# Post-norm multiplication of the last MLP quarter on GpSimd, and the last product's weight forms emitted earlier, in a two-layer decoder trunk

## The chip, the cores and the metric

One core of a Trainium2 chip. The metric is the time of one execution on the device, in microseconds (us), as the median of several executions; the profile is of one execution more.

## What is computed

Two layers of a decoder trunk on 512 tokens of width 1024, all in f32. Each layer is a token mixer (two attention groups on one input projection), a cross-attention into 256 memory tokens and an MLP, and each of the three has a norm in front and a norm behind, the latter added to the residual. The change lies in the last of the three and in what follows it:

```python
def rms_norm(x, g):
    y = xf * lax.rsqrt(jnp.mean(xf * xf, axis=-1, keepdims=True) + EPS)
    return (y * g.astype(jnp.float32)).astype(x.dtype)
...
for l in range(DEPTH):
    ...
    hdn = jnp.square(jax.nn.relu(rms_norm(x, pre_mlp_g[l]) @ w_up[l]))
    x = x + rms_norm(hdn @ w_down[l], post_mlp_g[l])
```

`w_up` is 1024 x 4096 and `w_down` 4096 x 1024.

## The kernel before

Every f32 matmul is made of three matmuls of a shorter type: each operand is split into a high part and a low rest (`whi` and `wlo` for weights, `fh` and `fl` for hidden values, `xth` and `xtl` for normalised tokens). ScalarE writes the high part, VectorE subtracts it from the source to get the rest. A raw weight tile `raw` holds two row blocks of 512 columns, so its split takes one ScalarE and one VectorE instruction of 1024 columns (L164, L165); weights of an input projection are also scaled by a norm's vector (L192, L197). There are 8 buffers for `raw` and 5 each for `whi` and `wlo`.

The tokens are 4 tiles of 128 rows (`t` from 0 to 3), the width is 2 halves of 512 columns (`n` 0 and 1). The MLP runs over 4 quarters of the hidden width (`qd_`). A quarter first computes its hidden values, then multiplies them with `w_down` by a scheme of seven products in place of eight. Product `p` needs a left form (sums of hidden blocks, `left_forms`) and two right forms, one for each `g` (differences of weight tiles, `right_form`: for product 4 one VectorE subtraction of 1024 columns at L1039, and then the split). A product is 24 matmuls into two PSUM tiles (`wa`, `wc` or `we`, one for each `j`), and `finish` adds these on VectorE into the accumulators `acc[t][n]` (L1107). In the last quarter the products run in the order 1, 2, 5, 6, 3, 7, 4:

```python
plan = ((1, A, True, False, ((0, 0),)), (2, E, True, True, ((0, 0),)),
        (5, C, True, False, ((2, 1),)), (6, A, False, False, ((0, 1),)),
        (3, C, False, True, ((0, 1),)), (7, A, False, True, ((2, 1), (2, 0))),
        (4, E, True, True, ((2, 0),)))
```

There a half of a row tile is complete after product 2 (tiles 0 and 1, left half), 3 (tiles 0 and 1, right), 7 (tiles 2 and 3, right) and 4 (tiles 2 and 3, left). `done(t, n)` then takes the sum of squares of the half on ScalarE (L372, tile `junk`) and multiplies the half by the post-norm's vector `gb[n]`, a 128x512 tile (L1045). When both halves of a tile are there, `add_post_norm` forms `pnm` from the two sums (L420, VectorE), raises it to the power -0.5 on GpSimd (`pnr`, L139; called the root below) and adds the scaled halves to the residual `xs` (L423, VectorE). In the last layer these go to the output; in the first they are stored in DRAM and normalised for the next layer (`norm_x`: squares, a root `n1r`, and `xn` on GpSimd and ScalarE), transposed on TensorE (`tp`) and used by the next input projection (`ptm`).

The right forms of the last product are made in a list of their own, `last_w`, after the matmuls of product 7 in the program's text.

The order in which each engine runs its instructions is set by the scheduler of the language from the program's text: an earlier place in the text gives priority, and an instruction that can't run yet lets others pass. Each engine then runs its own list strictly in order.

Of the kernel before, what the change touches and what calls it, by code (L numbers as in the profile page):

```python
# [16 lines left out]
OP = mybir.AluOpType  # L17
# [6 lines left out]
NT = S // 128  # L24
# [21 lines left out]
def block_kernel(ctx: ExitStack, tc, x, mem, positions, rel_bias, w_in, q_norm_g, w_uq, kv_norm_g,  # L46
# [3 lines left out]
    nc = tc.nc  # L50
# [38 lines left out]
    def store_x(t, dst):  # L89
        for n in range(2):  # L90
            nc.sync.dma_start(dst[t * 128:(t + 1) * 128, n * 512:(n + 1) * 512], xs[t][n])
# [274 lines left out]
    def feat_major(*a, **k):  # L366
        run(feat_major_steps(*a, **k))

    def sumsq(src, ss, scale=1.0):
        w = src.shape[-1]  # L370
        junk = unit("junk", (128, w))
        nc.scalar.activation(junk, src, AF.Square, scale=scale, accum_out=ss)  # L372
# [20 lines left out]
    def norm_x(h, lo, t, tag, help=None):  # L393

        hv = (h[:, 0:4, :], h[:, 4:8, :])
        lv = (lo[:, 0:4, :], lo[:, 4:8, :]) if SPLIT else (None, None)
        ms = small(tag + "ms", 2)
        for n in range(2):
            sumsq(xs[t][n], ms[:, n:n + 1], scale=1.0 / 32.0)
        r = row_rstd((ms[:, 0:1], ms[:, 1:2]), tag)  # L400
        xns = []
        for n in range(2):
            xn = unit("xn")
            if n == 1 and help is nc.scalar:
                nc.scalar.activation(xn, xs[t][n], AF.Copy, scale=r[:, 0:1])
            else:
                eng = nc.gpsimd if n == 0 or help is None else help
                eng.tensor_scalar(xn, xs[t][n], r[:, 0:1], 1.0, op0=OP.mult, op1=OP.mult)
            xns.append(xn)
        put_off(("xt", t), DELAY, lambda: [transposed(xns[n], n, list(zip(hv, lv)), t) for n in range(2)])  # L410

    def new_xt():
        h = xtp.tile([128, NK, S], WD, tag="xt", name="xth")
        l = xtp.tile([128, NK, S], WD, tag="xt", name="xtl") if SPLIT else None
        return h, l

    def add_post_norm(ys, ms, t, dst=None):

        m = small("pnm", 1)
        nc.vector.scalar_tensor_tensor(m, ms[:, 0:1], EPS, ms[:, 1:2], op0=OP.add, op1=OP.add)  # L420
        r = rpow(m, "pn")
        for n in range(2):
            nc.vector.scalar_tensor_tensor(xs[t][n], ys[n], r[:, 0:1], xs[t][n], op0=OP.mult, op1=OP.add)  # L423
            if dst is not None:
                (nc.sync, nc.scalar)[n].dma_start(dst[t * 128:(t + 1) * 128, n * 512:(n + 1) * 512], xs[t][n])
# [136 lines left out]
    for l in range(DEPTH):  # L562
# [437 lines left out]
        acc = [[None, None] for _ in range(NT)]  # L1000
        ss = [small("mss", 2) for _ in range(NT)]
        nxh = nxl = None
        gb = None

        def left_forms(F, ra, rb):

            a11, a21 = ra[:, :, 0:256], ra[:, :, 256:512]
            a12, a22 = rb[:, :, 0:256], rb[:, :, 256:512]

            def part(p, src):  # L1010
                h, lo = unit("fh", (128, 2, 256), WD), unit("fl", (128, 2, 256), WD)
                split_from(h, lo, src)
                F[p].append((h, lo))

            s1, s2 = unit("s1", (128, 2, 256)), unit("s2", (128, 2, 256))
            part(1, a11)
            nc.vector.tensor_add(s1, a21, a22)
            part(5, s1)
            nc.vector.tensor_sub(s2, s1, a11)
            part(6, s2)  # L1020
            part(2, a12)
            nc.vector.tensor_sub(a21, a11, a21)
            part(7, a21)
            nc.vector.tensor_sub(a12, a12, s2)
            part(3, a12)
            part(4, a22)
# [15 lines left out]
        def done(t, n):  # L1042

            sumsq(acc[t][n], ss[t][:, n:n + 1], scale=1.0 / 32.0)
            nc.vector.tensor_mul(acc[t][n], acc[t][n], gb[n])  # L1045
            ready_halves[t] += 1
            if ready_halves[t] < 2:
                return
            add_post_norm(acc[t], ss[t], t, out[0] if l == DEPTH - 1 else None)
            if l < DEPTH - 1:  # L1050
                store_x(t, xsave)
                norm_x(nxh, nxl, t, "n1", help=nc.scalar)
# [3 lines left out]
        for qd_ in range(4):  # L1056
            if qd_ == 3 and l < DEPTH - 1:
                nxh, nxl = new_xt()
            F = {p: [] for p in range(1, 8)}
            for g in range(2):  # L1060
                ra = pp.tile([128, 1280], F32, tag="P", name="ra", bufs=2)[:, 0:1024]
                rb = pp.tile([128, 1280], F32, tag="PT", name="rb", bufs=2)[:, 0:1024]
                ra, rb = [r.rearrange("p (k c) -> p k c", k=2) for r in (ra, rb)]

                def ev_up(m, ps, ra=ra, rb=rb):
                    r = (ra, rb)[m // 2][:, m % 2, :]
                    nc.scalar.activation(r, ps, AF.Relu)
                    nc.scalar.activation(r, r, AF.Square)

                feat_major(w_up[l], (qd_ * 2 + g) * 512, 4, NK, G_MLP + 8 * l, xh_f, xl_f, S, ev_up,  # L1070
                           whole=2 if qd_ == 0 and g == 0 else 0)
                left_forms(F, ra, rb)
            B = [[raw_w(w_down[l], qd_ * 1024 + g * 512 + r * 256, 2, n * 512, 512)
                  for r in range(2) for n in range(2)] for g in range(2)]
            A = [pss.tile([128, 512], F32, tag="s", name="wa") for _ in range(2)]
            C = [pst.tile([128, 512], F32, tag="t", name="wc") for _ in range(2)]
            E = [None] * 2
            end = qd_ == 3


            plan = ((1, A, True, False, ((0, 0),)), (5, C, True, False, ((2, 1),)),
                    (6, A, False, False, ((0, 1),)), (2, E, True, True, ((0, 0),)),
                    (7, A, False, False, ((2, 1),)), (3, C, False, True, ((0, 1),)),
                    (4, A, False, True, ((2, 0),)))
            if end:
# [4 lines that stand above are left out]
            for p, ps, first, last, dsts in plan:  # L1090
                if ps is E:
                    E[:] = [mm_ps("we") for _ in range(2)]

                def product(g, i, j, w):
                    c = slice(j * 128, (j + 1) * 128)
                    fh, fl = F[p][g]
                    mm(ps[j], fh[:, i, c], fl[:, i, c], w[0][:, i, :], w[1][:, i, :],
                       first and g + i == 0, g + i == 2, not first)

                def finish(j):  # L1100
                    for d, n in dsts:
                        t = d + j
                        if acc[t][n] is None:
                            acc[t][n] = unit("acc")
                            nc.vector.tensor_copy(acc[t][n], ps[j])  # L1105
                        else:
                            nc.vector.tensor_add(acc[t][n], ps[j], acc[t][n])  # L1107
                        if end and p in (2, 3, 4) or end and p == 7 and n == 1:
                            done(t, n)

                if end and p == 4:
                    for j in range(2):
                        for g in range(2):
                            for i in range(2):
                                product(g, i, j, last_w[g])
                        finish(j)
                        flush()
                    continue
                for g in range(2):
                    w = right_form(p, B[g])  # L1120
                    for i in range(2):
                        for j in range(2):
                            product(g, i, j, w)
                if end and p == 7:
                    last_w = [right_form(4, B[g]) for g in range(2)]
                if end and p == 1:
                    gb = row_bcast(post_mlp_g, l)
                for j in range(2):
                    finish(j)
                if end and p in (2, 5):  # L1130
                    for t in ((0, 1) if p == 2 else (2, 3)):
                        load_x(t, xmid)
                flush()
# [37 lines left out]
```

## Time and profile before

| | us |
|---|---|
| median of 3 runs (lowest to highest) | 1547.85 (1546.98 to 1550.19) |
| the profiled execution | 1551.81 |
| its span, first to last instruction | 1550.0 |
| TensorE busy | 1509.1 (97%) |
| VectorE busy | 995.9 (64%) |
| ScalarE busy | 820.0 (53%) |
| GpSimd busy | 239.0 (15%) |
| share of the chain that ended last: PE, DVE, POOL | 84%, 7%, 1% |

PE is TensorE, DVE VectorE, ACT ScalarE, POOL GpSimd, SP the engine that issues most transfers. A busy share is over the whole span. The chain that ended last is followed back from the last instruction, at each step to what released it.

### The profile page before, as it was taken

Reading aid. Unit: us, or ns where it says so; the run is one execution under the profiler, and the core shown is the slowest. Engines: PE = TensorE matmul, PEld = TensorE weight load, DVE = VectorE, ACT = ScalarE, POOL = GpSimd, SP = SyncE. Lnnn points to the kernel's source line nnn. Section 1 sums busy time; section 2 is a strip of 40 time slices with the busy share of each in tenths; the row PEclk is TensorE's granted clock in tenths of the full one; section 3 lists DMA queues with packets and bytes.
Section 4 is the critical chain, followed back from the end, with each engine's and each line's share of the span. In section 5 each row is a group of like instructions: output and inputs, shape, how many; then the busy total and the mean of one; then the engine's idle time right before and its main releaser. Section 6 shows DMA issues by size and latency. Waiting matters only on the chain.

```text
span 1550.0 us, 21290 instructions
## 1 busy us (share of the span) xinstructions
PE 1509.1 (97%) x7861; PEld 1265.6 (82%) x7861; DVE 995.9 (64%) x1780; ACT 820.0 (53%) x1578; POOL 239.0 (15%) x429
## 2 busy tenths in 40 slices
PE   8999999999999999999989999999999999999996
PEld 7777788898898888888868877978988988888885
DVE  5555775456458668585974667664654594958678
ACT  5355666346346464545554566653553654646363
POOL 2133631021020000000011355201111100000000
PEclk9989999999999999999999999999999999999999
DMA  6432223613131505151541322244322324060612
GB/s 235 143 116 69 79 65 109 204 55 119 53 114 50 181 28 177 41 166 59 179 131 51 122 81 91 69 140 145 109 82 68 115 71 155 17 195 20 190 55 82
DMA packets 87404, 164.09 MB, mean 106 GB/s; under 512 B 6230, under 2 KB 12036, under 8 KB 87300
## 3 DMA queue, kind: packets, MB, share of 16 engines
q1 hardware_dynamic: 86724, 161.68, 32.4%
q8 instruction: 62, 1.02, 0.3%
q10 hardware_dynamic: 576, 1.05, 0.2%
q14 instruction: 42, 0.34, 0.1%
HBM read 154.29 MB, written 11.03 MB: 107 GB/s over the span
## 4 chain that ended last, share of the span: by engine, by line
PE 84%; DVE 7%; issue 3%; ACT 2%; DMA 2%; POOL 1%; SPq 0%; DVEq 0%; POOLq 0%; ACTq 0%
PE pfm L240 12%; PE pfm L239 12%; PE pfm L241 12%; PE ptm L239 6%; PE ptm L240 6%; PE ptm L241 6%; PE wa L239 3%; PE wa L240 3%; PE wa L241 3%; PE sp L467 3%; PE op L230 3%; DVE wlo L197 2%; PE ptp L224 2%; PE wc L240 2%; PE wc L239 2%
## 5 line engine op out<-in xcount | busy, mean ns | idle before, releaser
L240 PE MATMUL pfm<-xth,wlo 128*128 128x512 f32 (+1 forms) x896 | 322.4, 360 | 0.6
L239 PE MATMUL pfm<-xtl,whi 128*128 128x512 f32 (+1 forms) x896 | 322.2, 360 | 0.0
L241 PE MATMUL pfm<-xth,whi 128*128 128x512 f32 (+1 forms) x896 | 321.6, 359 | 0.0
L197 DVE SCALAR_TENSOR_TENSOR wlo<-raw,gT,whi 128x512 fp32r<-128x512 f32 (+3 forms) x332 | 229.1, 729 | 131.6 <-ACT whi L192 129.9
L192 ACT ACTIVATE whi<-raw,gT 128x512 fp32r<-128x512 f32 (+2 forms) x324 | 209.2, 697 | 180.3 <-PE pfm L241 87.3
L164 ACT ACTIVATE whi<-raw 128x1024 fp32r<-128x1024 f32 x112 | 118.1, 1060 | 142.9 <-PE pfm L241 52.8
L240 PEld LDWEIGHTS pfm<-xth,wlo 128*128 128x128 f32 x896 | 169.2, 189 | 26.8 <-DVE wlo L197 1.4
L241 PEld LDWEIGHTS pfm<-xth,whi 128*128 128x128 f32 x896 | 169.2, 189 | 25.6 <-issue 0.5
L239 PEld LDWEIGHTS pfm<-xtl,whi 128*128 128x128 f32 x896 | 169.2, 189 | 24.8
L165 DVE TENSOR_TENSOR wlo<-raw,whi 128x1024 fp32r<-128x1024 f32 x112 | 134.8, 1217 | 34.3 <-ACT whi L164 34.3
L139 POOL TENSOR_TENSOR pnr<-pnm,mhalf 128x1 f32<-128x1 f32 x24 | 18.0, 750 | 828.8 <-DVE pnm L420 828.8
L475 POOL TENSOR_SCALAR P<-P,rs 128x128 f32<-128x128 f32 (+3 forms) x128 | 71.5, 563 | 151.6 <-DVE rs L474 81.2
L239 PE MATMUL wa<-wlo,fh 128*128 128x512 f32 x240 | 93.6, 390 | 0.5 <-DVE acc L1105 0.5
L241 PE MATMUL wa<-whi,fh 128*128 128x512 f32 x240 | 93.4, 389 | 0.0
L240 PE MATMUL wa<-whi,fl 128*128 128x512 f32 x240 | 93.4, 389 | 0.0
L473 ACT ACTIVATE P<-P,nm 128x128 f32<-128x128 f32 (+3 forms) x128 | 71.2, 557 | 34.1 <-DVE nm L471 33.4
L185 DVE TENSOR_TENSOR wlo<-raw,whi 128x1024 fp32r<-128x1024 f32 x32 | 39.1, 1222 | 59.3 <-ACT whi L184 58.6
L239 PE MATMUL ptm<-wlo,xth 128*128 128x512 f32 (+2 forms) x192 | 68.6, 359 | 3.4 <-DVE wlo L197 2.5
L184 ACT ACTIVATE whi<-raw 128x1024 fp32r<-128x1024 f32 x32 | 33.9, 1061 | 67.3 <-PE ptm L241 60.2
L240 PE MATMUL ptm<-whi,xtl 128*128 128x512 f32 (+2 forms) x192 | 67.1, 349 | 0.6 <-DVE xtl L203 0.6
L241 PE MATMUL ptm<-whi,xth 128*128 128x512 f32 (+2 forms) x192 | 66.3, 346 | 0.0
L224 PE MATMUL ptp<-ident,P 128*128 128x128 f32 x320 | 50.5, 282 | 3.9 <-ACT PT L494 2.3
(249 smaller groups left out, 3280.4 us busy)
## 6 DMA issues: line engine op xcount, KB each, us to landing
raw<-in_w_up SPq DMA_DIRECT2D x64, 512.0 KB, 4.6
raw<-in_w_down SPq DMA_DIRECT2D x64, 512.0 KB, 4.3
raw<-in_w_in SPq DMA_DIRECT2D x24, 512.0 KB, 5.5
raw<-in_w_xk SPq DMA_DIRECT2D x16, 512.0 KB, 5.4
raw<-in_w_xv SPq DMA_DIRECT2D x16, 512.0 KB, 3.6
raw<-in_w_mix_out SPq DMA_DIRECT2D x16, 512.0 KB, 4.7
raw<-in_w_xq SPq DMA_DIRECT2D x16, 512.0 KB, 6.4
raw<-in_w_xo SPq DMA_DIRECT2D x16, 512.0 KB, 4.1
```

Source lines behind the costliest of these rows:

```text
L164: nc.scalar.activation(hi, raw, AF.Copy)
L165: nc.vector.tensor_sub(lo, raw, hi.bitcast(F32))
L192: weight_parts[:] = [nc.scalar.activation(cols(hi, k, False), cols(raw, k, True), AF.Copy, scale=g).ins]
L197: nc.vector.scalar_tensor_tensor(lv, rv, g, hv, op0=OP.mult, op1=OP.subtract)
L224: ins = nc.tensor.transpose(out_, in_, ident_)
L230: nc.tensor.matmul(ps, lhsT=lhsT, rhs=rhs, start=start, stop=stop)
L239: nc.tensor.matmul(ps, lhsT=lh, rhs=rl, start=first, stop=False, skip_group_check=more)
L240: nc.tensor.matmul(ps, lhsT=ll, rhs=rh, start=False, stop=False, skip_group_check=more)
L241: nc.tensor.matmul(ps, lhsT=lh, rhs=rh, start=False, stop=last, skip_group_check=more)
L467: nc.tensor.matmul(sp[:, :L], lhsT=q[:, i * 128:(i + 1) * 128], rhs=k[:, :L], start=n == 0, stop=n == len(parts) - 1)
L473: nc.scalar.activation(Pi, Pi, AF.Exp, bias=nm[:, i:i + 1], scale=-1.0, accum_out=rs[:, i:i + 1])
L475: nc.gpsimd.tensor_scalar(Pi, Pi, rs[:, i:i + 1], 1.0, op0=OP.mult, op1=OP.mult)
```

## The change

```diff
         def done(t, n):
 
             sumsq(acc[t][n], ss[t][:, n:n + 1], scale=1.0 / 32.0)
-            nc.vector.tensor_mul(acc[t][n], acc[t][n], gb[n])
+            eng = nc.gpsimd if (t, n) != (NT - 1, 0) else nc.vector
+            eng.tensor_tensor(acc[t][n], acc[t][n], gb[n], op=OP.mult)
             ready_halves[t] += 1
@@
                             product(g, i, j, w)
-                if end and p == 7:
+                if end and p == 3:
                     last_w = [right_form(4, B[g]) for g in range(2)]
```

Of the eight multiplications of a layer, seven go to GpSimd; that of tile 3's left half stays on VectorE. The two right forms of product 4 are emitted after the matmuls of product 3, ahead of its `finish`. The lines behind move by one (L1045 becomes L1046, L1107 becomes L1108).

VectorE in the last layer, from the second form of product 6 on. `raw<-raw` is the subtraction for a form of 4, `wlo` a form's rest, `acc<-wa` and `acc<-wc` the adds of a product. Before:

```order
L1045 TENSOR_TENSOR acc<-acc,gb 128x512 x2
L165 TENSOR_TENSOR wlo<-raw,whi 128x1024 x2
L1107 TENSOR_TENSOR acc<-wa,acc 128x512 x2
L165 TENSOR_TENSOR wlo<-raw,whi 128x1024 x2
L1039 TENSOR_TENSOR raw<-raw 128x1024
L1107 TENSOR_TENSOR acc<-wc,acc 128x512 x2
L165 TENSOR_TENSOR wlo<-raw,whi 128x1024
L1045 TENSOR_TENSOR acc<-acc,gb 128x512
L420 SCALAR_TENSOR_TENSOR pnm<-mss 128x1
L1045 TENSOR_TENSOR acc<-acc,gb 128x512
L423 SCALAR_TENSOR_TENSOR xs<-acc,pnr,xs 128x512 x2
L420 SCALAR_TENSOR_TENSOR pnm<-mss 128x1
```

and with the change:

```order
L1039 TENSOR_TENSOR raw<-raw 128x1024
L165 TENSOR_TENSOR wlo<-raw,whi 128x1024 x2
L1108 TENSOR_TENSOR acc<-wa,acc 128x512 x2
L165 TENSOR_TENSOR wlo<-raw,whi 128x1024
L1039 TENSOR_TENSOR raw<-raw 128x1024
L1108 TENSOR_TENSOR acc<-wc,acc 128x512
L165 TENSOR_TENSOR wlo<-raw,whi 128x1024
L420 SCALAR_TENSOR_TENSOR pnm<-mss 128x1
L1108 TENSOR_TENSOR acc<-wc,acc 128x512
L423 SCALAR_TENSOR_TENSOR xs<-acc,pnr,xs 128x512 x2
L420 SCALAR_TENSOR_TENSOR pnm<-mss 128x1
L165 TENSOR_TENSOR wlo<-raw,whi 128x1024
```

The first pair of `wlo` is product 3's in both. After the `wa` adds, the old order has the two forms of product 7 and then those of 4; the new one has the two forms of 4, and the first form of 7 behind the `xs` adds of tile 0. The second form of 7 follows behind the `xs` adds of tile 1.

GpSimd at the same place, from the last normalisations of the cross-attention to the end. Before:

```order
L408 TENSOR_SCALAR xn<-xs,n3r 128x512 x2
L139 TENSOR_TENSOR pnr<-pnm,mhalf 128x1
L139 TENSOR_TENSOR n3r<-n3m,mhalf 128x1
L408 TENSOR_SCALAR xn<-xs,n3r 128x512 x2
L139 TENSOR_TENSOR pnr<-pnm,mhalf 128x1 x4
```

and with the change:

```order
L408 TENSOR_SCALAR xn<-xs,n3r 128x512 x2
L1046 TENSOR_TENSOR acc<-acc,gb 128x512 x3
L139 TENSOR_TENSOR pnr<-pnm,mhalf 128x1
L1046 TENSOR_TENSOR acc<-acc,gb 128x512
L139 TENSOR_TENSOR pnr<-pnm,mhalf 128x1
L1046 TENSOR_TENSOR acc<-acc,gb 128x512 x3
L139 TENSOR_TENSOR pnr<-pnm,mhalf 128x1 x2
```

The four roots of the last norm now stand behind three, one, three and no multiplications.

TensorE at the end of the last layer, with buffer numbers: `wa` is product 7, `we` product 4. Before, where 7 ends and 4 begins:

```order
L239 MATMUL wa_14068<-wlo_14314,fh_14038 128x512
L240 MATMUL wa_14068<-whi_14313,fl_14039 128x512
L241 MATMUL wa_14068<-whi_14313,fh_14038 128x512
L239 MATMUL we_14349<-wlo_14331,fh_13871 128x512
L240 MATMUL we_14349<-whi_14330,fl_13872 128x512
L241 MATMUL we_14349<-whi_14330,fh_13871 128x512
```

and with the change, the last six:

```order
L239 MATMUL wa_14068<-wlo_14324,fh_14038 128x512
L240 MATMUL wa_14068<-whi_14323,fl_14039 128x512
L241 MATMUL wa_14068<-whi_14323,fh_14038 128x512
L239 MATMUL we_14350<-wlo_14278,fh_14047 128x512
L240 MATMUL we_14350<-whi_14277,fl_14048 128x512
L241 MATMUL we_14350<-whi_14277,fh_14047 128x512
```

Product 7's 24 matmuls stood ahead of all of product 4; now 21 of product 4's stand ahead of product 7, and three behind it. The first layer is ordered in the same way, with 20 and 4.

## Rows read from the trace of the kernel before

**Rows 1.** The page: its span, and busy time of TensorE, weight loads, VectorE, ScalarE, GpSimd.
```profile
span 1550.0 us, 21290 instructions
PE 1509.1 (97%) x7861; PEld 1265.6 (82%) x7861; DVE 995.9 (64%) x1780; ACT 820.0 (53%) x1578; POOL 239.0 (15%) x429
```
**Rows 2.** Busy time by stretch: change of layer, and end.
```profile
core 0: us, PE busy (x) PEld busy (x) DVE busy (x) ACT busy (x) POOL busy (x), PEclk, DMA share, GB/s
...
770.00:790.00 20.00, 14.72 (x63) 10.65 (x62) 18.62 (x34) 16.72 (x39) 6.87 (x9) 0.91 0.57 185
...
1505.00:1550.00 45.00, 33.09 (x144) 26.43 (x142) 38.99 (x56) 15.92 (x29) 3.87 (x4) 0.92 0.27 94
```
**Rows 3.** Timeline of TensorE, change of layer: start, us, operation, [idle before <-what ended it].
```profile
779.12 1.09 PE L224 MATMUL tp<-ident,xn 128*128 128x128 f32 x8 [2.37 <-POOL xn L408]
...
785.07 0.50 PE L239 MATMUL ptm<-wlo,xth 128*128 128x512 f32 x1 [2.01 <-DVE wlo L197]
...
788.35 0.63 PE L240 MATMUL ptm<-whi,xtl 128*128 128x512 f32 x1
```
**Rows 4.** Timeline of TensorE, product 4 of the last layer.
```profile
1532.21 0.39 PE L239 MATMUL we<-wlo,fh 128*128 128x512 f32 x1
...
1534.71 0.39 PE L241 MATMUL we<-whi,fh 128*128 128x512 f32 x1
1536.18 0.50 PE L239 MATMUL we<-wlo,fh 128*128 128x512 f32 x1 [1.09 <-DVE wlo L165]
...
1538.81 0.39 PE L241 MATMUL we<-whi,fh 128*128 128x512 f32 x1
```
**Rows 5.** Timeline of VectorE, end of the last layer.
```profile
1517.84 1.29 DVE L1045 TENSOR_TENSOR acc<-acc,gb 128x512 f32<-128x512 f32 x2
1519.04 2.35 DVE L165 TENSOR_TENSOR wlo<-raw,whi 128x1024 fp32r<-128x1024 f32 x2
...
1531.92 1.22 DVE L1039 TENSOR_TENSOR raw<-raw 128x1024 f32<-128x1024 f32 x1
...
1534.91 1.22 DVE L165 TENSOR_TENSOR wlo<-raw,whi 128x1024 fp32r<-128x1024 f32 x1
...
1545.06 1.42 DVE L423 SCALAR_TENSOR_TENSOR xs<-acc,pnr,xs 128x512 f32<-128x512 f32 x2 [0.67 <-POOL pnr L139]
```
**Rows 6.** Groups by line on GpSimd, shapes apart: one input tile (count, busy us, mean ns).
```profile
L408 POOL TENSOR_SCALAR xn<-xs,n2r 128x512 f32<-128x512 f32 x16 | 11.9, 755 | 0.8
```
**Rows 7.** Line 601, two input tiles on GpSimd: ns, lowest/median/highest.
```profile
L601 POOL TENSOR_TENSOR qst<-ra,rb x16: 453/462/525, 157.1 to 954.6; 128x128 f32<-128x128 f32 x16
...
L601 POOL TENSOR_TENSOR ckv<-ra,rb x8: 250/258/263, 134.6 to 899.3; 128x32 f32<-128x32 f32 x8
```
**Rows 8.** Timeline of GpSimd, two pairs of normalisations in the first layer.
```profile
312.83 1.37 POOL L408 TENSOR_SCALAR xn<-xs,n2r 128x512 f32<-128x512 f32 x2
...
325.06 1.80 POOL L408 TENSOR_SCALAR xn<-xs,n2r 128x512 f32<-128x512 f32 x2
```
**Rows 9.** Timeline of VectorE: three forms beside the second pair, and three others.
```profile
325.48 2.58 DVE L197 SCALAR_TENSOR_TENSOR wlo<-raw,gT,whi 128x512 fp32r<-128x512 f32 x3
...
809.96 2.07 DVE L197 SCALAR_TENSOR_TENSOR wlo<-raw,gT,whi 128x512 fp32r<-128x512 f32 x3
```
**Rows 10.** Timeline of GpSimd, two roots at the end of the last layer.
```profile
1532.08 1.46 POOL L139 TENSOR_TENSOR pnr<-pnm,mhalf 128x1 f32<-128x1 f32 x1 [1.60 <-DVE pnm L420]
...
1544.48 0.55 POOL L139 TENSOR_TENSOR pnr<-pnm,mhalf 128x1 f32<-128x1 f32 x1 [1.59 <-DVE pnm L420]
```
**Rows 11.** Timeline of ScalarE: the sums of squares of tiles 0 and 1, left half.
```profile
1516.44 0.19 ACT L372 ACTIVATION_READ_ACCUMULATOR junk<-acc 128x1 f32 x1
...
1517.06 0.19 ACT L372 ACTIVATION_READ_ACCUMULATOR junk<-acc 128x1 f32 x1
```
**Rows 12.** Timeline of VectorE, change of layer.
```profile
779.68 1.92 DVE L1045 TENSOR_TENSOR acc<-acc,gb 128x512 f32<-128x512 f32 x3
...
784.27 0.74 DVE L197 SCALAR_TENSOR_TENSOR wlo<-raw,gT,whi 128x512 fp32r<-128x512 f32 x1
```

## The prediction

> **What bounds the kernel now.** First the page's busy times: TensorE is busy 97% of the 1550.0 us span, VectorE 64%, GpSimd 15% [rows 1]. That is a mean; the change touches only the last quarter of each layer's MLP, so the second view is busy time by stretch [rows 2]. At the change of layer TensorE works 14.72 us of 20 at a granted clock of 0.91, with VectorE at 18.62; in the last 45 us TensorE works 33.09 and VectorE 38.99. **There VectorE sets the pace**, and the third view, the timeline of each engine, shows how. TensorE stands 2.37 us for a normalised tile and 2.01 us for a weight form; after that its matmuls take 0.63 instead of 0.39, the half clock [rows 3, 4]. At the very end it waits 1.09 us for the last form of product 4 [rows 4]. That form (1534.91) stands on VectorE behind the adds into `xs` of tiles 0 and 1, and after TensorE's last matmul (1538.81) VectorE still has adds, multiplications and the root's round trip to GpSimd, so that its last `xs` pair starts at 1545.06 [rows 4, 5]. So a gain has to come out of VectorE's queue, and whatever holds VectorE or lengthens the trip to GpSimd is a loss.
>
> **Taken off VectorE.** Seven of eight multiplications per layer: 0.60 us each from start to start (a pair takes 1.29, of which 0.69 is the later one's whole duration [rows 5]), 4.2 us per layer.
>
> **Put on GpSimd.** The trace has no multiplication of 128x512 by a second tile there. Nearest from below: the same size with one input tile takes 0.755 [rows 6]. Two inputs at smaller sizes: 0.258 for 32 columns, 0.462 for 128 [rows 7], 2.13 ns a column, so 0.258 + 480 x 0.00213 = **1.28 us** for 512; this has the same form and I take it. From above: four times the 128-column row, 1.85. The Trainium skill (GPSIMD Engine Reference, section 3.1, Elementwise) states 4497 ns for a two-input add of 2048 columns; a quarter is an estimate of 1.12, by which the sum below would be +5.2 instead of +7.4; no run here shows that size.
>
> **GpSimd and VectorE are not independent.** A pair of normalisations on GpSimd alone takes 1.37, beside VectorE's two-input forms 1.80 [rows 8]; three such forms take 2.07, beside that pair 2.58 [rows 9]. Both got longer, VectorE by 0.51. A root on GpSimd takes 0.55 when VectorE stands still and 1.46 beside its subtraction of two weight tiles at 1531.92; it ends 0.4 after that (1533.54 against 1533.14) [rows 5, 10]. So I let the two take turns: a multiplication's 1.28, less 0.2 of start, keeps VectorE's two-SBUF-input instructions out and the reverse; adds from PSUM go on. The 0.2 is my choice: with 0.75 in its place the sum is +5.3. The Trainium skill (SBUF, State Buffer, section Who interferes with whom) says that one of the two then fully blocks until the other's instruction is over, without such a start; by that the sum would be +8.5. The 0.51 above is on the short side of that rule, since two whole normalisations would cost more.
>
> I carried the new order through with these durations: VectorE 1.14 for 1024 columns, 0.60 and 0.67 for 512 [rows 5], matmuls 0.227 (eleven steps from 1532.21 to 1534.71) [rows 4], an instruction starting when its engine is free and its inputs are there. The old order carried through in the same way starts its last `xs` add at 1545.49, where the trace has 1545.73 (half of the pair at 1545.06) [rows 5]; such a walk is good to some tenths.
>
> **Last layer, up to TensorE's last matmul.**
> - The squares of tiles 0 and 1 end at 1516.63 and 1517.25 [rows 11]. Both go to GpSimd at once, where VectorE is in a row of two-input instructions. In turn: form of 6, multiplication, subtraction for 4, multiplication, form of 3. The first form of 3, ended by 1520.18 before (1519.04 + 1.14 [rows 5]), comes at 1522.15, product 3 is due at 1521.33: **+0.82**.
> - Product 4 goes ahead of product 7 on TensorE. Its second form is ready at 1529.17, due at 1528.95: +0.22. The old wait of 1.09 [rows 4] is gone: **-1.08** (walk).
> - Product 7's forms are now the late ones. They stand on VectorE behind the `xs` adds of tile 0, which wait for the root, and the root stands on GpSimd behind tile 0's right half: multiplied 1529.52 to 1530.80, root until 1531.40, first add until 1532.07, second held by tile 1's multiplication until 1533.69. Form of 7 at 1535.03, due at 1532.57: **+2.45**; the second one +0.16.
> Together +2.57: the last matmul starts at 1541.76 instead of 1539.19.
>
> **Last layer, from there to the end.** Before 6.30 us from the last matmul to the start of the last `xs` add. Now product 7 ends with TensorE's row, so six adds from PSUM follow it (until 1543.78). GpSimd takes three halves in a row of 1.28, at 1541.65, 1542.95 and 1544.25, and only then the root of tile 2: 1546.13. Two adds, the one multiplication left on VectorE (0.60), the last root, 1548.92; the last add starts at 1549.59, 7.83 after the last matmul: **+1.53**. Layer's sum **+4.10**. The stores behind it are the same two.
>
> **First layer.** The same three waits before product 7, 0.80 + 0.22 + 1.67. Then the next layer's normalisations wait for roots behind multiplications: waits of 2.00, 1.53, 3.17, 0.33 and 1.18 in the walk. Together 10.90, where the old order's walk has 7.57: **+3.33**. On the plus side, the form for which TensorE waits 2.01 stands behind three multiplications of 1.92 on VectorE [rows 3, 12], and these leave; the walk has that in. The half-clocked stretch (eight matmuls 0.2 longer, 1.7) I leave as it is, since idle stays as long. Behind it TensorE runs without a wait, so this carries to the end.
>
> DMA: the same transfers; SP's stores of `xs` move ahead of three weight loads, whose forms are wanted some 20 us later: nothing. Making the form of 4 early costs no instruction.
>
> **Sum: +3.33 + 4.10 = +7.4 us.** The profiled execution took 1551.81, 3.96 above the median of the runs, 1547.85; so 1559.2 against it, and **1555.3** as a median. With the unknown durations at their ends: 0.755 gives +0.9 (-0.9 if nothing blocks), 1.85 gives +15.3.
>
> **Rivals.** A measurement tells about 0.2%, 3.1 us.
> - A, the forecast: 1.1 to 1.6 us a multiplication, in turns: +5.0 to +11.8, 1552.9 to 1559.7. For it: [rows 7 to 10]. Chance 0.60.
> - B, no turns: the lengthened forms had another cause, a multiplication holds VectorE up nowhere and only the roots' queue on GpSimd counts: +0.8 + 2.2, 1550.9. Against it: both engines grew at the same moment. 0.15.
> - C, faster: GpSimd multiplies at the one-input rate (two in 1.37, 0.69 each [rows 8]) beside VectorE, without turns. Then the walk gives -2.1 at the change of layer and +0.8 at the end; TensorE's idle there falls so far that the half clock (1.7) goes too: -3.1, **1544.8**. It decides itself where a multiplication takes under 0.7. For it: VectorE really is the busiest engine there. Against it: [rows 7]. 0.12.
> - D, worse: 1.85 a multiplication, or the longer idle brings further half-clocked stretches: 1563.2. 0.13.
> That nothing moves is out: the order has seven multiplications per layer on GpSimd and product 4 ahead of 7.
>
> **How the numbers follow.** Time 1555.3, from A. The range takes in B and A, down to 1547.0 (0.755 without blocking) and up to 1562 (1.6 us and one more half-clocked stretch, +13.5): it leaves out C and most of D, 0.2 in all. Faster: most of C, 0.10. Same: half of B, the low edge of A and the rest of C, 0.15. Slower: 0.75.
>
> **What would show it.** GpSimd's multiplications: about 1.28 alone, about 2.1 at 1516 in the place of the two at 1517.84; VectorE's subtraction or form beside them about 2.1 instead of 1.22. TensorE: waits at products 3 and 7 in both layers, 0.22 at most before 4. At the end three multiplications in a row before tile 2's root. If multiplications take 0.7 and forms beside them stay at 1.22, C is right; if they take 1.3 and the forms stay, B. If the last `xs` add doesn't start near 7.8 us after TensorE's last matmul, the tail was mis-sized; if the layer change loses nothing, the walk through it was.

## The result, and the profile after

| | before | after |
|---|---|---|
| median of 6 runs each on one chip (lowest to highest), us | 1549.02 (1546.98 to 1552.38) | 1557.37 (1556.70 to 1560.69) |
| ratio, with its 95% interval | | 1.0054 (1.0039 to 1.0069) |
| the profiled execution, us | 1551.81 | 1556.81 |

The change makes the kernel slower by 8.4 us (0.0054 x 1549.02; the interval is 6.0 to 10.7). Forecast was +7.4, as a median 1555.3 against 1547.85; "slower" had 0.75.

The page of the changed kernel, span and busy times, as in [rows 1]:

```profile
span 1555.0 us, 21286 instructions
...
PE 1507.8 (97%) x7861; PEld 1261.8 (81%) x7861; DVE 994.8 (64%) x1766; ACT 820.0 (53%) x1578; POOL 259.9 (17%) x443
```

Fourteen instructions left VectorE (1780 to 1766) and came to GpSimd (429 to 443), where they cost 20.9 us. VectorE lost only 1.1 us of busy time, though 14 multiplications of 0.60 are 8.4: that is the first sign that its other instructions got longer. The same shows by stretch, as in [rows 2], at the change of layer and at the end:

```profile
core 0: us, PE busy (x) PEld busy (x) DVE busy (x) ACT busy (x) POOL busy (x), PEclk, DMA share, GB/s
...
770.00:790.00 20.00, 14.76 (x67) 11.28 (x65) 16.77 (x28) 13.68 (x31) 12.78 (x12) 0.91 0.59 193
...
1510.00:1555.00 45.00, 29.39 (x124) 22.70 (x123) 33.63 (x43) 13.37 (x25) 13.89 (x11) 0.92 0.21 74
```

The granted clock at the change of layer is 0.91 as before; TensorE is no busier there, GpSimd takes 12.78 of 20 us instead of 6.87.

**Where the time went.** The profiled execution can be cut at marks that both kernels have on VectorE: the first add of product 5 in each layer's last quarter, the fourth copy out of the next layer's projection (L660), and the start of the last `xs` pair.

| piece, us | before | after | difference |
|---|---|---|---|
| start to product 5, first layer | 753.17 | 749.99 | -3.18 |
| from there through the change of layer (fourth copy) | 56.19 | 59.44 | **+3.25** |
| second layer up to product 5 | 706.05 | 706.47 | +0.42 |
| from there to TensorE's last matmul | 23.40 | 26.28 | **+2.88** |
| from there to the start of the last `xs` pair | 6.25 | 7.60 | **+1.35** |
| the rest | 4.94 | 5.22 | +0.28 |

These add up to the 5.0 by which the span grew. The first row has the same instructions in both kernels; it scatters from execution to execution (last section), so the three bold pieces are compared below, and the medians for the sum. The pieces are of one profiled execution of each kernel.

Timeline of GpSimd at the end of the last layer:

```profile
1517.19 4.60 POOL L1046 TENSOR_TENSOR acc<-acc,gb 128x512 f32<-128x512 f32 x2 [300.32 <-DMA xs<-xmid]
1530.34 1.29 POOL L1046 TENSOR_TENSOR acc<-acc,gb 128x512 f32<-128x512 f32 x1 [8.55 <-issue]
1531.60 0.55 POOL L139 TENSOR_TENSOR pnr<-pnm,mhalf 128x1 f32<-128x1 f32 x1
1532.11 1.28 POOL L1046 TENSOR_TENSOR acc<-acc,gb 128x512 f32<-128x512 f32 x1
...
1542.77 3.72 POOL L1046 TENSOR_TENSOR acc<-acc,gb 128x512 f32<-128x512 f32 x3 [6.55 <-ACT junk L372]
1546.45 0.55 POOL L139 TENSOR_TENSOR pnr<-pnm,mhalf 128x1 f32<-128x1 f32 x1
```

and of VectorE, the place of [rows 5]:

```profile
1517.19 1.22 DVE L165 TENSOR_TENSOR wlo<-raw,whi 128x1024 fp32r<-128x1024 f32 x1
1518.32 2.32 DVE L1039 TENSOR_TENSOR raw<-raw 128x1024 f32<-128x1024 f32 x1
1520.56 3.45 DVE L165 TENSOR_TENSOR wlo<-raw,whi 128x1024 fp32r<-128x1024 f32 x2
...
1530.32 0.68 DVE L1108 TENSOR_TENSOR acc<-wc,acc 128x512 f32<-128x512 f32 x1
1532.18 2.43 DVE L423 SCALAR_TENSOR_TENSOR xs<-acc,pnr,xs 128x512 f32<-128x512 f32 x2 [1.18 <-POOL pnr L139]
...
1534.60 1.21 DVE L165 TENSOR_TENSOR wlo<-raw,whi 128x1024 fp32r<-128x1024 f32 x1
...
1547.03 1.41 DVE L423 SCALAR_TENSOR_TENSOR xs<-acc,pnr,xs 128x512 f32<-128x512 f32 x2 [1.75 <-POOL pnr L139]
...
1549.78 1.41 DVE L423 SCALAR_TENSOR_TENSOR xs<-acc,pnr,xs 128x512 f32<-128x512 f32 x2 [0.66 <-POOL pnr L139]
```

Read the two side by side. A multiplication takes 1.29 at 1530.34, where VectorE runs an add from PSUM (1530.32, 0.68: neither is longer than it is elsewhere) and then stands idle. The two at 1517.19 take 2.30 each, and in the same time VectorE's subtraction for a form of 4 takes 2.32 instead of 1.22 [rows 5], and the two forms behind it 3.45 instead of 2.35 [rows 5]: 1.10 longer each time. From 1530.34 on the order in GpSimd's queue shows: multiplication, then tile 0's root, and only then VectorE's `xs` adds, which waited 1.18; the first of the two adds is held by the next multiplication, which starts just ahead of it (1532.11) and takes 1.28: the pair takes 2.43 instead of 1.41. Product 7's form stands behind them, at 1534.60. At the end three multiplications stand ahead of tile 2's root, and VectorE waits 1.75 for it.

TensorE's timeline, the first matmuls behind those waits, and its last one:

```profile
757.03 0.50 PE L239 MATMUL wc<-wlo,fh 128*128 128x512 f32 x1 [0.96 <-DVE wlo L165]
...
768.90 0.50 PE L239 MATMUL wa<-wlo,fh 128*128 128x512 f32 x1 [1.36 <-DVE wlo L165]
...
778.17 0.51 PE L239 MATMUL ptm<-wlo,xth 128*128 128x512 f32 x1 [1.72 <-ACT xth L201]
...
780.08 1.09 PE L224 MATMUL tp<-ident,xn 128*128 128x128 f32 x4 [1.40 <-DVE xtl L203]
...
1522.93 0.50 PE L239 MATMUL wc<-wlo,fh 128*128 128x512 f32 x1 [0.95 <-DVE wlo L165]
...
1535.87 0.50 PE L239 MATMUL wa<-wlo,fh 128*128 128x512 f32 x1 [2.21 <-DVE wlo L165]
...
1542.18 0.39 PE L241 MATMUL we<-whi,fh 128*128 128x512 f32 x1
```

The wait before product 4 [rows 4] is gone; in its place stand one before product 3 (0.95) and one before product 7 (2.21) in the last layer, and 0.96 and 1.36 at the same two places in the first. In the last layer these come to 2.07 more than before, and the piece grew by 2.88: the other 0.8 stands in no listed wait. Some of it is in short gaps: right behind a wait matmuls start up to 0.34 apart instead of 0.23, and the second forms of products 4 and 7 come some 0.1 late (matmuls at 1529.97 and 1538.86).

### The profile page after: what moved, and what is told of

Read it like the earlier page. It is cut to its first block, busy times and chain, and to the rows that moved or that the text cites. A ratio compares the mean times of both kernels' runs of the same rounds, so it can differ in the third digit from the quotient of the medians.

```text
span 1555.0 us, 21286 instructions
## 1 busy us (share of the span) xinstructions
PE 1507.8 (97%) x7861; PEld 1261.8 (81%) x7861; DVE 994.8 (64%) x1766; ACT 820.0 (53%) x1578; POOL 259.9 (17%) x443
## 3 DMA queue, kind: packets, MB, share of 16 engines
q8 instruction: 62, 1.02, 0.3%
## 4 chain that ended last, share of the span: by engine, by line
PE 79%; DVE 9%; issue 4%; ACT 3%; POOL 2%; DMA 2%; SPq 0%; DVEq 0%; POOLq 0%; ACTq 0%
PE pfm L240 12%; PE pfm L239 12%; PE pfm L241 12%; PE ptm L239 6%; PE ptm L240 6%; PE ptm L241 6%; PE op L230 3%; PE sp L467 3%; PE wa L239 3%; PE wa L240 3%; PE wa L241 3%; DVE wlo L197 2%; PE ptp L224 2%; DVE wlo L165 1%; DMA tb<-tabw 1%
## 5 line engine op out<-in xcount | busy, mean ns | idle before, releaser
L1046 POOL TENSOR_TENSOR acc<-acc,gb 128x512 f32<-128x512 f32 x14 | 22.3, 1611 | 625.0 <-ACT junk L372 307.5
L239 PEld LDWEIGHTS wa<-wlo,fh 128*128 128x128 f32 x240 | 45.0, 188 | 15.5 <-DVE wlo L165 4.8
```

The source lines that it names most:

```text
L239: nc.tensor.matmul(ps, lhsT=lh, rhs=rl, start=first, stop=False, skip_group_check=more)
```

## The experiments

Each was timed beside the kernel before, in two sessions on one chip each: the kernel before had 1550.45 as its median in the first (29 runs; the first four kernels below), 1549.79 in the second (24; the last three). The diffs are against the changed kernel where nothing else is said. For all of them the three pieces of the table above, as differences to before, from one profiled execution each:

| kernel | change of layer | to last matmul | tail | sum | ratio (95% interval) |
|---|---|---|---|---|---|
| the change | +3.25 | +2.88 | +1.35 | +7.5 | 1.0054 (1.0039 to 1.0069) |
| early forms alone | +3.14 | -0.42 | +2.51 | +5.2 | 1.0038 (1.0026 to 1.0050) |
| GpSimd alone | +2.47 | +2.53 | -0.29 | +4.7 | 1.0046 (1.0030 to 1.0063) |
| one input on GpSimd | -1.19 | -0.07 | +0.74 | -0.5 | 1.0004 (0.9992 to 1.0017) |
| writes alone on GpSimd | -1.36 | -0.96 | +0.54 | -1.8 | 0.9996 (0.9986 to 1.0005) |
| forms of 7 and 4 early | -1.40 | -1.39 | -0.45 | -3.2 | 0.9979 (0.9967 to 0.9990) |
| the same, seven on GpSimd | +4.19 | -0.14 | +2.37 | +6.4 | 1.0039 (1.0024 to 1.0055) |
| the same, two on GpSimd | -1.60 | -1.39 | -0.54 | -3.5 | 0.9977 (0.9962 to 0.9992) |

For each kernel the sum of the pieces lies within the interval of its ratio. The piece left out, the second layer up to product 5, moved between -0.34 (early forms alone) and +3.65 (forms of 7 and 4 early), as the last section tells.

**The two parts apart.** First the early forms without GpSimd:

```diff
-            eng = nc.gpsimd if (t, n) != (NT - 1, 0) else nc.vector
+            eng = nc.vector
```

> The early weight forms alone; all eight multiplications of a layer back on VectorE. Theory (GpSimd's multiplications and VectorE's two-input instructions take turns, and product 7's forms come late behind the residual adds): slower than before by 3.1 us, 1.0 at the change of layer and 2.1 at the end, since the order of products alone already makes product 7's forms late; VectorE's subtraction for product 4 beside nothing, 1.22 us. Rival 1 (only GpSimd's own queue counts, nothing is blocked): the same +3, as nothing is on GpSimd. Rival 2 (the order of the products is the whole loss): +8. If the early forms are a help by themselves: below 0.

Measured: 1555.17 (1551.31 to 1559.33), ratio 1.0038. The end of the last layer came out as expected: TensorE waits 0.3 in all there, but now it ends with product 7, and six adds from PSUM and four multiplications follow on VectorE: the tail grows by 2.51. The change of layer cost 3.14 where 1.0 was expected. TensorE's waits there, largest first:

```profile
PE tp L224 <- DVE xtl L203: 3.6, 1, 3.6
PE tp L224 <- POOL xn L408: 1.9, 1, 1.9
PE ptm L239 <- ACT xth L201: 1.5, 1, 1.5
```

and its stretches, in the columns of [rows 2]:

```profile
770.00:790.00 20.00, 14.90 (x69) 12.04 (x68) 18.29 (x33) 14.81 (x34) 7.88 (x9) 0.83 0.62 198
790.00:810.00 20.00, 18.06 (x77) 14.81 (x76) 8.73 (x15) 5.82 (x12) 2.75 (x3) 0.91 0.25 80
```

The granted clock is 0.83 and 0.91 here; before it is 0.91 [rows 2] and 1.00 in the same two windows:

```profile
790.00:810.00 20.00, 20.00 (x98) 16.65 (x96) 12.21 (x21) 8.84 (x17) 1.25 (x2) 1.00 0.39 112
```

A mean clock lower by 0.08 and 0.09 over 20 us each is full-speed work of at most 3.4 us fewer; in part of that time TensorE stands idle anyway. It could hold the 2.1 that the expectation lacks, but no run kept the waits and took the half clock (1.2 GHz) away, so it isn't shown.

Then GpSimd without the early forms:

```diff
-                if end and p == 3:
+                if end and p == 7:
                     last_w = [right_form(4, B[g]) for g in range(2)]
```

> Seven multiplications per layer on GpSimd; the weight forms of product 4 where they were. Theory (turns): +3.8 us, 1.5 at the change of layer and 2.4 at the end, VectorE's forms and subtractions up to 2.3 us beside a multiplication. Rival 1 (queue only): about -0.2. Rival 2 (order of products): 0.

Measured: 1558.01 (1553.01 to 1560.95), ratio 1.0046. TensorE's waits at the end of the last layer:

```profile
PE we L239 <- DVE wlo L165: 2.4, 1, 2.4
PE wc L239 <- DVE wlo L165: 1.0, 1, 1.0
```

The wait before product 3 (1.0) is there without the early forms, so it belongs to the multiplications; the one before product 4, 1.09 before [rows 4], grows to 2.4. This also speaks against rival B, which had this kernel at about -0.2. Each part alone is a loss of about 5 us in the pieces, both together 7.5: they don't add up (9.9). At the end of the last layer they do (2.09 and 2.24 apart, 4.23 together), though the multiplications that leave VectorE shorten the tail that the early forms make (2.51 to 1.35). The difference lies at the change of layer (3.14 and 2.47 apart, 3.25 together), and no run shows why. In the medians GpSimd alone costs 7.1 us (4.7 to 9.8), which can't be told from the change itself.

**Why GpSimd's multiplications hold VectorE.** The next two kernels keep work for the same seven halves per layer on GpSimd and change what it is. One has a single input tile, a multiplication by a constant one, with the vector left out:

```diff
-            eng = nc.gpsimd if (t, n) != (NT - 1, 0) else nc.vector
-            eng.tensor_tensor(acc[t][n], acc[t][n], gb[n], op=OP.mult)
+            if (t, n) != (NT - 1, 0):
+                nc.gpsimd.tensor_scalar(acc[t][n], acc[t][n], mhalf[:, 0:1], -2.0, op0=OP.mult, op1=OP.mult)
+            else:
+                nc.vector.tensor_tensor(acc[t][n], acc[t][n], gb[n], op=OP.mult)
```

> The changed kernel, with GpSimd's seven multiplications per layer done by a constant 1 in place of the post-norm's vector, so that they read one tile (the vector is left out there). Theory: about 0.69 us each in place of 1.29; the loss falls from 7.4 to about +0.1 us (-0.9 at the change of layer, +1.0 at the end). Rival 1 (queue only, nothing blocked): -1.4. Rival 2 (order of products): +8, as the order stays.

Measured: 1551.38 (1545.48 to 1554.49), ratio 1.0004: no change against before that can be told. The first two on GpSimd, and one of them later:

```profile
1515.73 5.52 POOL L1046 TENSOR_SCALAR acc<-acc,mhalf 128x512 f32<-128x512 f32 x2 [300.33 <-ACT junk L372]
...
1538.39 0.69 POOL L1046 TENSOR_SCALAR acc<-acc,mhalf 128x512 f32<-128x512 f32 x1 [6.55 <-ACT junk L372]
```

VectorE at that moment:

```profile
1515.73 1.22 DVE L165 TENSOR_TENSOR wlo<-raw,whi 128x1024 fp32r<-128x1024 f32 x1
1516.86 1.22 DVE L1039 TENSOR_TENSOR raw<-raw 128x1024 f32<-128x1024 f32 x1
1518.00 2.77 DVE L165 TENSOR_TENSOR wlo<-raw,whi 128x1024 fp32r<-128x1024 f32 x2
```

Beside VectorE's adds from PSUM (at 1538.39) it takes 0.69, yet beside VectorE's two-input instructions two take 5.52: they take turns too, and here GpSimd does most of the waiting. So a multiplication at 0.69 would have removed the loss and brought no gain that can be told: the gain of rival C needed both the rate and no turns.

The other kernel writes the half twice with constants and reads nothing, so fourteen instructions per layer; the multiplication of those halves is left out:

```diff
-            eng = nc.gpsimd if (t, n) != (NT - 1, 0) else nc.vector
-            eng.tensor_tensor(acc[t][n], acc[t][n], gb[n], op=OP.mult)
+            if (t, n) != (NT - 1, 0):
+                for v in (0.5, 1.0):
+                    nc.gpsimd.memset(acc[t][n], v)
+            else:
+                nc.vector.tensor_tensor(acc[t][n], acc[t][n], gb[n], op=OP.mult)
```

> The changed kernel, with each of GpSimd's seven multiplications per layer replaced by two fills of the same half with a constant (the multiplication is left out there): they occupy GpSimd for about 1.0 us together, but read nothing. Theory (turns between instructions that read): VectorE's subtraction and forms beside them stay at 1.22 us, and the kernel is 1.9 us faster than before (-1.6 and -0.3). Rival 1 (the queue on GpSimd is what costs): most of the loss stays, about +5, and VectorE's instructions are as long as before anyway. Any GpSimd instruction in the way of VectorE: forms of 1.7 us or more beside the fills.

Measured: 1550.06 (1546.84 to 1550.94), ratio 0.9996. GpSimd, the four writes for tiles 0 and 1:

```profile
1515.31 2.16 POOL L1047 MEMSET acc<- 128x512 f32 x4 [300.31 <-ACT junk L372]
```

VectorE beside them:

```profile
1515.32 1.22 DVE L165 TENSOR_TENSOR wlo<-raw,whi 128x1024 fp32r<-128x1024 f32 x1
1516.45 1.22 DVE L1039 TENSOR_TENSOR raw<-raw 128x1024 f32<-128x1024 f32 x1
1517.59 2.35 DVE L165 TENSOR_TENSOR wlo<-raw,whi 128x1024 fp32r<-128x1024 f32 x2
```

Two writes take 1.08, near the 1.28 of a multiplication, at the same place and in the same queue; VectorE's instructions keep 1.22, and the writes keep 0.54. So it is the reading of tiles by both engines that makes them longer, and neither that GpSimd is busy nor the order of its queue. (The writes are also another kind of instruction; that reading is what counts, and not some other difference, rests on this run and on the one-input run, whose instruction reads and does get longer.) The Trainium skill (SBUF — State Buffer, section Who interferes with whom) has this: a VectorE instruction with two inputs from SBUF gets in the way of a GpSimd one that reads SBUF, and not of one that only writes. The rows of this run agree (1.22 beside writes, 2.32 beside multiplications). In the pieces this kernel gains 1.8 us. Its median doesn't tell that apart from none: -0.6, with an interval of -2.2 to +0.8. Against the early forms alone, with which it shares the early forms, it is 7.0 us better in the pieces (-1.8 against +5.2): as an estimate from these two runs, that is about what VectorE without seven multiplications would be worth if the engines didn't take turns.

**What would help.** With the forms of 4 early, product 7's forms are the late ones, behind the `xs` adds. So both forms of 7 were made early as well, and all multiplications left on VectorE:

```diff
-            eng = nc.gpsimd if (t, n) != (NT - 1, 0) else nc.vector
+            eng = nc.gpsimd if False else nc.vector
@@
-                    w = right_form(p, B[g])
+                    w = seven[g] if end and p == 7 else right_form(p, B[g])
@@
                 if end and p == 3:
+                    seven = [right_form(7, B[g]) for g in range(2)]
                     last_w = [right_form(4, B[g]) for g in range(2)]
```

> All multiplications on VectorE, and the forms of product 7 emitted ahead of product 3's finish as well, in front of the early forms of product 4. Theory (the early forms of 4 cost because product 7's forms fall behind the residual adds of tiles 0 and 1, and product 7's adds then all come at the end): the loss of the early forms turns into a gain, -2.5 us against before (-1.5 at the change of layer, -1.0 at the end). Rival (forms of 4 early are a loss by themselves, as they fill VectorE's queue): still +3 or more.

Measured: 1546.90 (1544.45 to 1550.86), ratio 0.9979 (0.9967 to 0.9990): faster than the kernel before by 3.3 us (1.5 to 5.1). The rival, that early forms of 4 are a loss by themselves, falls with that. VectorE in the last layer:

```profile
1523.27 2.35 DVE L165 TENSOR_TENSOR wlo<-raw,whi 128x1024 fp32r<-128x1024 f32 x2
...
1528.42 2.35 DVE L165 TENSOR_TENSOR wlo<-raw,whi 128x1024 fp32r<-128x1024 f32 x2
...
1532.10 1.41 DVE L423 SCALAR_TENSOR_TENSOR xs<-acc,pnr,xs 128x512 f32<-128x512 f32 x2
...
1543.99 1.41 DVE L423 SCALAR_TENSOR_TENSOR xs<-acc,pnr,xs 128x512 f32<-128x512 f32 x2 [0.66 <-POOL pnr L139]
```

The pair at 1523.27 is product 7's, the one at 1528.42 product 4's: all four stand ahead of the first `xs` add (1532.10). TensorE waits for nothing in the last layer from product 5's adds on, and product 4 is its last again, so the tail is short (5.80). At the change of layer its list of waits has one line left, for the next layer's normalised tiles:

```profile
PE tp L224 <- POOL xn L408: 4.8, 2, 4.0
```

The same with the change's seven multiplications on GpSimd; the diff is against the kernel just shown:

```diff
-            eng = nc.gpsimd if False else nc.vector
+            eng = nc.gpsimd if (t, n) != (NT - 1, 0) else nc.vector
```

> As the run with both forms early, and seven multiplications per layer on GpSimd as in the change. Theory: the order of the forms is mended, the turns and GpSimd's queue are left: +4.9 us against before (2.5 and 2.4). Rival (order of products is the cause): as fast as the run with both forms early, -2.5.

Measured: 1556.17 (1554.49 to 1560.43), ratio 1.0039: the multiplications on GpSimd cost 9.7 us in the pieces (from -3.24 to +6.42), although the forms are early. So the order of the products is not the whole loss. Its first layer is worse than was expected (+4.19 for 2.5). The list of TensorE's waits there comes to 8.2 us against 5.3 before, 3.9 of them in two waits for VectorE's rests of normalised tiles (`xtl`). The granted clock is 0.95 from 770 to 790 us and 0.88 from 790 to 810, against 0.91 and 1.00 before. No run separates the waits from the clock, so how much is due to which stays open.

Last, two multiplications alone on GpSimd, picked so that no root stands close behind them (tile 1's left half, tile 2's right half); the diff is against the kernel just shown:

```diff
-            eng = nc.gpsimd if (t, n) != (NT - 1, 0) else nc.vector
+            eng = nc.gpsimd if (t, n) in ((1, 0), (2, 1)) else nc.vector
```

> As the run with both forms early, with only two multiplications per layer on GpSimd: tile 1's left half and tile 2's right half. Theory: these two lie where VectorE adds from PSUM and where no root waits behind them, so a little is gained on top: -3.2 us (-2.0 and -1.2). If a multiplication on GpSimd costs wherever it stands: 0 or above.

Measured: 1546.44 (1544.12 to 1550.69), ratio 0.9977 (0.9962 to 0.9992). GpSimd's two in the last layer:

```profile
1517.69 1.77 POOL L1046 TENSOR_TENSOR acc<-acc,gb 128x512 f32<-128x512 f32 x1 [300.93 <-ACT junk L372]
...
1535.75 1.80 POOL L1046 TENSOR_TENSOR acc<-acc,gb 128x512 f32<-128x512 f32 x1 [0.81 <-ACT junk L372]
```

They take 1.8 each beside VectorE, so they still meet it, but the next root on GpSimd comes 12.18 and 3.18 us after them. In the pieces it is 0.3 better than the version without GpSimd; the medians (1546.44 and 1546.90) can't tell the two apart. Both are faster than the kernel before and than the change.

## Why the prediction was right, point by point

- **VectorE sets the pace, and what holds it is a loss.** The mechanism is right: the two places named are the two that grew, +3.25 at the change of layer (forecast +3.33) and +4.23 at the end (forecast +4.10); all the rest of the second layer moved by 0.42.
- **A multiplication's price.** Forecast 1.28 from the two smaller shapes [rows 7]; the median of the fourteen is 1.296 (group of the line on GpSimd: lowest 1.266, highest 2.375):

```profile
L1046 POOL TENSOR_TENSOR acc<-acc,gb x14: 1266/1296/2375, 751.3 to 1545.2; 128x512 f32<-128x512 f32 x14
```

  The estimate of 1.12 from the Trainium skill (GPSIMD Engine Reference, section 3.1, Elementwise) is 0.18 too low. [rows 7] suggests why: by its two shapes an instruction has a fixed part of 0.19 us (0.258 - 32 x 0.00213), and a quarter of a long instruction's time holds only a quarter of that, 0.14 too little.
- **Turns.** Forecast that a two-input instruction of VectorE is held for 1.08 of the 1.28; the rows show 1.10 (2.32 against 1.22, 3.45 against 2.35). Multiplications there took 2.30 where about 2.1 was forecast. Adds from PSUM went on, as forecast (1530.32). The run with writes alone shows the cause. The held time is 0.18 less than the multiplication's 1.28, near the 0.2 of the forecast; that 0.2 was a choice which no row of before gave, so that it fits so closely is luck. By the rule of the Trainium skill (SBUF — State Buffer, section Who interferes with whom), one engine blocked for the other's whole instruction, the sum was +8.5; the pieces give +7.5, and the medians (+8.4, 6.0 to 10.7) can't tell the two sums apart. It is the 1.10 in the rows that speaks for the shorter hold.
- **Up to the last matmul.** Forecast +2.57 (0.82 before product 3, -1.08 before 4, 2.45 before 7); measured +2.88, with listed waits of 0.95 before 3, none before 4 and 2.21 before 7, and the rest in no listed wait. Of the adds into `xs` it is the first that is held at 1532.18, where the walk had the second.
- **The tail.** Forecast 7.83 from the last matmul to the last `xs` add, measured 1542.18 to 1550.45 (half of the last pair), 8.27; before 6.92, where the walk had 6.30. The walk was short by 0.4 to 0.6 in both orders, and the difference came out. As a difference to before +1.35 (forecast +1.53). The run with early forms alone shows that product 7 standing last on TensorE makes this, as the text had it, and the run with both forms early, where product 4 is last again, has the short tail back (-0.45). The multiplications there cost less on GpSimd, ahead of the root, than on VectorE (+1.35 against +2.51).
- **The change of layer.** The difference was right, the single waits were not all: 0.96 before product 3 and 1.36 before 7 for 0.80 and 1.67, but behind them no wait above 1.72 where the walk had 3.17. Its total of waits was longer for both kernels by 2 to 3 us than the lists of waits (10.90 and 7.57 against some 8.1 and 5.3; the lists leave short gaps out), and in the difference this cancels. That the difference is so close is luck in part: for the tried kernels the expectations at the change of layer missed by 2.1 (early forms alone), 1.7 (both forms early with seven on GpSimd) and 1.0 (GpSimd alone).
- **Rivals.** B (only the queue on GpSimd counts) falls with the 2.32 of VectorE's subtraction, with GpSimd alone, and with the writes, which stand in the same queue and cost nothing that can be told. How the change's loss divides between the turns and the roots behind the multiplications no run separates. C falls with the 1.296, and with the one-input run: at 0.69 there is no gain while the engines take turns. The half-clocked stretch that C let go stayed in every run: from 753 to 810 us the granted clock is 0.97 before and 0.91 to 0.97 in the others. D's further half-clocked stretches did not come in the change itself (0.91 at the change of layer, as before), but in the run with the early forms alone (0.83 and 0.91) and in the one with both forms early and seven on GpSimd (0.88 from 790 to 810 us) they did.

The step from pieces to median holds as well: +7.5 in one execution, +8.4 (6.0 to 10.7) in the medians.

## What to carry to other kernels

Before work goes from a busy VectorE to an idle GpSimd, look at what VectorE runs at that moment: where VectorE has two inputs from SBUF and the work on GpSimd reads SBUF too, the two waited for each other here, and the transfer buys less than its price (0.60 saved, 1.10 lost by VectorE for a multiplication beside it). Look also at what stands behind the moved work in GpSimd's queue, here the roots that VectorE waits for. And where an operand is made earlier, ask which one is then the latest: making the last product's forms early paid only once the product that it overtook had its forms early too.

## What was not expected

- **Who waits in the turns.** Beside multiplications, the two engines split the wait (for each of the two, GpSimd 2.30 - 1.28 = 1.02 and VectorE 1.10). Beside the one-input instruction GpSimd waited 4.1 for its two (5.52 less 2 x 0.69) and VectorE 0.42 (2.77 against 2.35). No run here shows what decides it.
- **Scatter far from the change.** From 0 to product 5 of the first layer all kernels run the same instructions, yet the eight profiled executions of the changed and tried kernels and the one of before take 749.5 to 754.7 us there. TensorE's clock in one early stretch differs. Before:

```profile
90.00:160.00 70.00, 63.74 (x350) 51.69 (x350) 38.13 (x131) 40.38 (x107) 24.14 (x57) 0.88 0.26 84
```

  and the kernel with both forms early and seven multiplications on GpSimd:

```profile
90.00:160.00 70.00, 63.23 (x372) 52.00 (x371) 39.20 (x133) 42.03 (x110) 26.66 (x62) 0.98 0.27 87
```

  At 0.98 instead of 0.88 TensorE gets 22 matmuls further in the same 70 us; this execution reaches product 5 at 749.52, the one of before at 753.17. The second layer up to product 5, the piece that the table of the experiments leaves out, scatters too: 705.72 to 709.71 us in the nine. The longest is the kernel with both forms early. Up to 43 us after the fourth copy all nine are alike to 0.1 us; the 3.65 us that it is behind the kernel before come after that, and from 850 to 900 us its granted clock is 0.93 where before has 1.00. With a scatter of 5.2 us in the first layer and 4.0 in the second, against 8.4 that this change costs, one execution's time can't judge it. Pieces cut at common marks leave this scatter out; how much the pieces themselves scatter no run shows, as each kernel has one profile.
